# Where a modulation product stands between the matmuls of a two-layer trunk, and how its token sums are formed

## The chip, the cores and the metric

The kernel runs on one core of a Trainium2 chip. The metric is the device time of one execution in microseconds (us). Five engines work side by side, each through its own list of instructions in order: PE (matrix products, with PEld for its weight loads), DVE (the vector engine), ACT (the scalar engine), POOL (GpSimd) and SP, which here does nothing but issue transfers from memory. An engine that waits for a semaphore holds everything behind it in its own list.

## The reference

Two layers of a diffusion trunk work on 512 latent tokens and 256 context tokens of width 1024. Each layer takes six modulation vectors from a small product, mixes the tokens (convolution branch and differential attention, one output projection), and then runs a squared-ReLU MLP of width 4096:

```python
mx = (silu_c @ w_ada[i] + b_ada[i])[:, None, :]      # latent: 6 x 1024 numbers
mc = silu_cc @ w_ada[i] + b_ada[i]                   # context: the same weights
sx1, ax1, gx1, sx2, ax2, gx2 = jnp.split(mx, 6, axis=-1)
...
x = x + gx1 * y_x
x = x + gx2 * sqrelu_mlp(modulate(rmsnorm(x, norm2_g[i]), sx2, ax2), w_mlp1[i], w_mlp2[i])
h_ctx = h_ctx + gc2 * sqrelu_mlp(modulate(rmsnorm(h_ctx, norm2_g[i]), sc2, ac2), w_mlp1[i], w_mlp2[i])
```

The modulation of layer 1 depends on the conditioning alone, not on the tokens. It can be computed at any time before layer 1 begins.

## The kernel before, in words

Every product is done in three matmuls (L140 to L142, in `mm3`, or L149 and L152 in the order "low half last"): an operand is split into a rounded high part and the rest, and high by high, high by low and low by high are added up in PSUM. So every weight slab and every activation has to be split before PE may use it: the high part by ACT (a copy that rounds), the low part by a subtraction on DVE or POOL. In the traces a name with `h` or `hi` is a high part and one with `l` or `lo` a low part.

This case lies between the end of layer 0's token mixing and the start of layer 1. The stages, in order:

- **Output projection** (tiles `o`): the merged branches times `w_out`, 24 blocks of 128 channels by 256 tokens. DVE adds each block to the residual stream `X` (L1395), ACT and DVE sum its squares (`nsq_so`, `acc`). Each 256 tokens ("half" in the code, three of them) are then normalized by `norm_mod`: PE sums over channels (`nc_n`), DVE and POOL form the reciprocal root (`ms_n`; the power is on POOL, L347), DVE or ACT puts it on a diagonal (`dg_n`), PE spreads it over the partitions (`nb_n`, L357), and DVE, ACT and POOL write the normalized `h2hh` and `h2hl`.
- **First features** (tiles `f_0`): the first 512 of the 4096 hidden units, from slabs `w1`, in 8 blocks over latent tokens and 4 over context tokens. ACT squares them (`hidden`, L1494 to L1496; context blocks go through a buffer `fr`, of which there is one), DVE takes the low part into `F` (L1499).
- **Second product** (tiles `r`) of chunk 0, then for chunks 1 to 6 a product of seven block products instead of eight (Strassen, for the latent and context tokens cut at token 384, tiles `p`) and again the second product (`second_slots`). Strassen needs sums of token blocks, `TS` and a new `h2h` block, made once in `token_sums`: chains of additions into a buffer `G` (L1509), each chain ended by a split (L77).
- **Features of chunk 7** (tiles `f_7`), then **out slabs**: the last second product over 1024 hidden units in 24 blocks of 256 tokens (tiles `r` again, L140 to L142), with sums of squares and the first normalization of layer 1 (`norm1`: `nc_n_1`, `ms_n_1`, `dg_n_1`, `nb_n_1`, `h1h`, `h1l`), and then `qk`, the first product of layer 1.

**The modulation of layer 1** is `ada_rows`, a generator whose steps are called one by one (`ada_step`, `ada`). It goes through 12 pairs of slabs of `w_ada`, numbered s = 0, 2, ... 22, each in 8 rows of 128x512. A row is loaded by SP (tile `ar`, 256 KB, L299), the first row is scaled by ACT (L312), the other seven are multiplied and added by DVE (L314, into `adaac`, later into a piece of `G`), once for s of 8 and more, twice below it (latent and context). A pair ends with a transpose and a reduction on DVE (L323, L325) into `part`, and after s = 6 and s = 22 PE folds `part` (`adaps`, L288). There are 112 operations of L314 in all. Before the change the rows are kept in two buffers, the generator is first called beside first features, and it runs to its end beside the out slabs. `part` lies in the buffer `dg` of the pool `spool`, of which there is one; `dg_n` uses the same buffer.

**What sets the order.** A scheduler places the instructions of each engine by its own cost model. Where code stands in `with in_order():`, each engine's instructions keep the order in which they are written; every such block starts anew. Inside the chunks a table `PACE` says how many modulation steps (or, in chunk 0, token sums) follow each half block.

## Time and profile before

| | |
|---|---|
| median of 3 runs | 2345.85 us (2343.96 to 2348.31) |
| the profiled execution | 2341.43 us, span from first to last instruction 2339.7 us |
| PE busy | 2240.5 us, 96% of the span |
| DVE, ACT, POOL busy | 72%, 45%, 28% |
| layer 0's output projection | about 750 to 818 us |
| first features | 818 to 857 us |
| second product of chunk 0 | from 863 us |
| features of chunk 7 | 1256 to 1290 us |
| out slabs and first normalization of layer 1 | 1290 to 1380 us |

A row of the timeline reads: start in us, duration in us, engine, source line, operation, output tile <- input tiles, shapes, count; in brackets at its end, for how long the engine had been idle and who ended that. A row of the stage table reads: stretch, its length, and busy time with the number of instructions for PE, PEld, DVE, ACT and POOL; then PEclk, the mean clock that PE was granted (1.00 is full), the share of the transfer engines in use, and GB/s. A row of the table of waits reads: engine, tile and line that waited, the engine, tile and line that released it, total in us, how often, the longest.

### The profile page before, as it was taken

What the parts mean: (1) busy time and instruction counts of PE and PEld (TensorE: products, weight loads), DVE (VectorE), ACT (ScalarE), POOL (GpSimd) and SP (SyncE); (2) the same over time, 40 slices, a digit from 0 to 9 for tenths busy, and PEclk for the clock granted to TensorE, in tenths of its full rate; (3) what the DMA queues carried; (4) which work ended last, traced back from release to release, by engine and by line L of the source; (5) the groups of instructions that cost most, each with busy time, mean ns of one, the idle gap of its engine ahead of it and who ended that gap; (6) DMA issues with size and microseconds to landing.
All of it is one profiled execution on the core that took longest, in us unless ns stands there. A gap on an engine that the chain in (4) does not pass through costs nothing.

```text
span 2339.7 us, 36471 instructions
## 1 busy us (share of the span) xinstructions
PE 2240.5 (96%) x14402; PEld 2024.9 (87%) x14402; DVE 1683.5 (72%) x2754; ACT 1053.4 (45%) x2049; POOL 643.8 (28%) x781
## 2 busy tenths in 40 slices
PE   8999999999999979999999978999998999999999
PEld 6999998888888969999999878999987879888887
DVE  6777776599666477788676567777759976757673
ACT  5555654522332353343346235555543333655542
POOL 1866764110000131222122238576621000100000
PEclk9999999999999989999999989999999999999999
DMA  9211111134535131233344541112113423442251
GB/s 309 64 41 33 45 46 45 46 129 158 174 126 178 48 122 37 91 99 122 100 126 152 171 110 55 40 30 62 44 59 110 137 83 127 153 127 90 73 180 36
DMA packets 202266, 232.62 MB, mean 99 GB/s; under 512 B 8864, under 2 KB 162928, under 8 KB 201968
## 3 DMA queue, kind: packets, MB, share of 16 engines
q1 hardware_dynamic: 202096, 230.30, 31.1%
q8 instruction: 113, 1.85, 0.3%
q14 instruction: 57, 0.47, 0.1%
HBM read 212.93 MB, written 17.35 MB: 98 GB/s over the span
## 4 chain that ended last, share of the span: by engine, by line
PE 71%; DVE 12%; ACT 6%; POOL 4%; issue 3%; DMA 3%; SPq 0%; DVEq 0%; POOLq 0%; ACTq 0%
PE r L149 5%; PE gt L140 3%; PE gt L141 3%; PE gt L142 3%; PE r L141 3%; PE r L142 3%; PE r L140 3%; PE r L152 3%; PE f L141 3%; PE f L142 3%; PE f L140 3%; PE qk L140 2%; PE qk L141 2%; PE qk L142 2%; PE yc L149 2%
## 5 line engine op out<-in xcount | busy, mean ns | idle before, releaser
L1197 DVE SCALAR_TENSOR_TENSOR cacc<-z,cols,cacc 128x783 f32<-128x783 f32 (+1 forms) x240 | 208.3, 924 | 0.3
L140 PE MATMUL qk<-h_wqk,h1h 128*128 128x256 f32 x640 | 184.6, 291 | 4.3 <-ACT h1h L379 2.2
L141 PE MATMUL qk<-l_wqk,h1h 128*128 128x256 f32 x640 | 181.7, 286 | 0.0
L142 PE MATMUL qk<-h_wqk,h1l 128*128 128x256 f32 x640 | 176.6, 286 | 0.0
L961 DVE TENSOR_REDUCE st<-S 128x1 f32<-128x768 f32 (+1 forms) x160 | 134.5, 846 | 56.8 <-PE S L959 55.7
L964 ACT ACTIVATE e<-S,st 128x768 f32<-128x768 f32 (+1 forms) x160 | 130.9, 821 | 41.6 <-DVE st L961 40.6
L141 PE MATMUL f<-h2hl,h_w 128*128 128x512 f32 (+1 forms) x416 | 143.3, 346 | 1.3 <-POOL h2hl L77 1.2
L140 PE MATMUL f<-h2hh,h_w 128*128 128x512 f32 (+1 forms) x416 | 142.1, 347 | 1.1 <-ACT h2hh L76 1.0
L142 PE MATMUL f<-h2hh,l_w 128*128 128x512 f32 (+1 forms) x416 | 142.4, 344 | 0.0
L140 PE MATMUL gt<-h1h,h_wg 128*128 128x512 f32 (+1 forms) x384 | 138.2, 360 | 0.0
L141 PE MATMUL gt<-h1l,h_wg 128*128 128x512 f32 (+1 forms) x384 | 136.6, 356 | 0.0
L142 PE MATMUL gt<-h1h,l_wg 128*128 128x512 f32 (+1 forms) x384 | 136.6, 356 | 0.0
L149 PE MATMUL r<-F,whir 128*128 128x512 f32 (+1 forms) x384 | 125.7, 343 | 7.5 <-ACT whir L1548 6.2
L140 PEld LDWEIGHTS qk<-h_wqk,h1h 128*128 128x128 f32 x640 | 123.9, 194 | 7.9 <-ACT h1h L379 3.6
L149 PE MATMUL r<-F,wlor 128*128 128x512 f32 (+1 forms) x384 | 125.4, 342 | 3.2 <-DVE wlor L1551 1.9
L141 PEld LDWEIGHTS qk<-l_wqk,h1h 128*128 128x128 f32 x640 | 124.1, 194 | 0.3 <-POOL l_wqk L77 0.3
L142 PEld LDWEIGHTS qk<-h_wqk,h1l 128*128 128x128 f32 x640 | 120.9, 194 | 0.0
L140 PE MATMUL v<-h_wv,h1h 128*128 128x256 f32 x384 | 111.5, 290 | 6.6 <-ACT rwc L853 3.3
L142 PE MATMUL v<-h_wv,h1l 128*128 128x256 f32 x384 | 109.2, 284 | 0.0
L141 PE MATMUL v<-l_wv,h1h 128*128 128x256 f32 x384 | 108.7, 283 | 0.0
L795 POOL TENSOR_TENSOR rqk<-rqk,mhalf 128x4 f32<-128x4 f32 x80 | 86.0, 1078 | 79.1 <-DVE rqk L794 77.9
L957 PE MATMUL S<-qk 128*128 128x512 f32 (+1 forms) x288 | 101.8, 357 | 5.3 <-ACT e L964 4.7
(399 smaller groups left out, 7465.4 us busy)
## 6 DMA issues: line engine op xcount, KB each, us to landing
r_w<-in_w_mlp_dram SPq DMA_DIRECT2D x34, 1024.0 KB, 5.4
ada<-in_w_ada_dram SPq DMA_DIRECT2D x24, 1024.0 KB, 5.7
ar<-in_w_ada_dram SPq DMA_DIRECT2D x96, 256.0 KB, 2.9
r_wg<-in_w_in_dram SPq DMA_DIRECT2D x16, 1024.0 KB, 5.2
r_wqk<-in_w_in_dram SPq DMA_DIRECT2D x30, 512.0 KB, 5.2
rf<-in_w_mlp_dram SPq DMA_DIRECT2D x26, 512.0 KB, 3.7
rr<-in_w_mlp_dram SPq DMA_DIRECT2D x24, 512.0 KB, 3.5
r_wao<-in_w_attn_out_dram SPq DMA_DIRECT2D x8, 1024.0 KB, 5.1
```

What stands on the lines that cost most here:

```text
L140: nc.tensor.matmul(ps, sh, mh, start=first, stop=False)
L141: nc.tensor.matmul(ps, sh, ml, start=False, stop=False)
L142: nc.tensor.matmul(ps, sl, mh, start=False, stop=last)
L149: nc.tensor.matmul(ps, w[j][:, k, m0 : m0 + P], a(k)[0][:, toks], start=k + j == 0, stop=False)
L152: nc.tensor.matmul(ps, w[0][:, k, m0 : m0 + P], a(k)[1][:, toks], start=False, stop=k == nk - 1)
L795: nc.gpsimd.tensor_tensor(out=r, in0=r, in1=mhalf[:, :4], op=ALU.pow)
L957: nc.tensor.matmul(S[:, o], QH[:, m, ts], QH[:, 2 + m, lo:hi], start=True, stop=False)
L961: nc.vector.tensor_reduce(out=st[:, m : m + 1], in_=S[:, :nkey], axis=AX.X, op=ALU.max, negate=True)
L964: nc.scalar.activation(out=e[:, :nkey], in_=S[:, :nkey], func=AF.Exp, bias=st[:, m : m + 1], accum_out=st[:, 2 + m : 3 + m])
L1197: nc.vector.scalar_tensor_tensor(out=ca[cc][:, :CV], in0=zt[cc][:, t : t + CV], scalar=wcol, in1=ca[cc][:, :CV], op0=ALU.mult, op1=ALU.add)
```

## The change

1. `ada_rows` takes a list `early` of slab pairs that go first, here s = 0 and s = 8. They are called beside the output projection, one step or two behind each of the first 15 of its 24 blocks (`ada_beside`), with three row buffers (tag `ar`). None is called beside first features any more. The other ten pairs keep two buffers, and start in chunk 1.
2. `part` gets tiles of its own (`adp2`, `adp1`), so it no longer shares the buffer of `dg_n`.
3. `token_sums` forms its sums in another way: the sum of a block's high and low part is kept and used again. 9 additions and 4 low parts per half of the channels, where there were 10 and 4.
4. All `in_order` blocks from first features to chunk 7 share one dictionary, so the order is pinned across them too.
5. In chunk 0 all four low parts of the second product's slabs (`wlor`) are on DVE; three of them were on POOL. Three of the four loads for them are issued before first features.
6. `PACE` and the counts of steps beside the features of chunk 7 and the out slabs are set anew.

```diff
@@ in_order
-    def in_order():
+    def in_order(before):
...
-        before = {}
@@ ada_rows
-        plan = [(s, k) for s in range(0, 24, 2) for k in range(8)]
+        plan = [(s, k) for s in (*early, *(s for s in range(0, 24, 2) if s not in early))
+                for k in range(KT)]
...
+            tag, bufs = ("ar", 3) if s in early else ("araw", 2)
+            r = state["tp"].tile([P, 512], F32, tag=tag, bufs=bufs, name=f"ar{i}_{s}_{k}")
...
-                    part = spool.tile([P, 4, P], F32, tag="dg", bufs=1, name=f"adp{i}_{s}")[:, :, :32]
+                    parts[nq] = state["xp"].tile([P, 4, 32], F32, tag=f"adp{nq}", bufs=1,
+                                                 name=f"adp{i}_{s}")
@@ output projection
+        def ada_beside(*counts):
+            left = list(counts)
+            def tick():
+                for _ in range(left.pop(0) if left else 0):
+                    with tc.issue_after(state["done"]):
+                        next(ada_todo, None)
+            return tick
...
+            ada_todo = ada_rows(i + 1, Ln, (0, 8))
...
-                  (lambda: mlp1_slab(0, 0), lambda: mlp1_slab(0, 1)))
+                  (lambda: mlp1_slab(0, 0), lambda: mlp1_slab(0, 1)),
+                  None if last else ada_beside(*[1] * 10, 2, 2, 2, 2, 1))
@@ token_sums
-                    yield from sums(g0, f32(b12[0]), (less, b11[0]), (plus, b12[1]), (less, b11[1]))
-                    yield from sums(g1, f32(b22[0]), (less, b12[0]), (plus, b22[1]), (less, b12[1]))
+                    yield from sums(g0, (plus, *b12))
+                    yield from sums(g1, (less, b22[0], g0), (plus, None, b22[1]))
+                    yield from sums(g0, (less, None, b11[0]), (less, None, b11[1]))
                     split(*t1, g0)
                     yield
-                    yield from sums(g0, g1, (plus, b11[0]), (plus, b11[1]))
+                    yield from sums(g0, (less, b22[0], None), (plus, None, b22[1]))
                     split(*t3, g1)
@@ first features
+            for half in ((0, 0), (0, 1), (1, 0)):
+                load("r", 0, *half)
...
-                        if n:
-                            ada_step()
...
-                        sum_step((4, 4, 2, 0)[2 * s + m])
+                        sum_step((4, 3, 0, 1)[2 * s + m])
...
                             r0.fill(0, nc.vector)
-                            r0.fill(1, nc.gpsimd)
+                            r0.fill(1, nc.vector)
@@ chunks, chunk 7 and out slabs
-            PACE = {0: [(1, 1), (1, 1), (1, 1), (1, 1), (1, 1), (1, 1), (1, 2), (2, 1)],
+            PACE = {0: [(1, 1), (1, 1), (2, 1), (2, 1), (0, 1), (1, 0), (1, 2), (1, 1)],
...
-                        own = (ada,) if c > 2 else ()
+                        own = (ada,) if c > 1 else ()
...
+                    eng = nc.gpsimd if c else nc.vector
...
-                            ada((2, 2, 2, 2, 2, 2, 1, 0)[n])
+                            ada((2, 2, 2, 2, 2, 2, 0, 0)[n])
...
-                gate2, f"r{i}", norm1, after, tick=ada_step, ahead=
+                gate2, f"r{i}", norm1, after, tick=ada_beside(2, 2, *[1] * 10), ahead=
```

Lines below the edits are shifted: L1499 becomes L1512, L1509 becomes L1522, L1551 becomes L1565, L314 becomes L321, L1395 becomes L1400.

DVE around the end of first features, before (`adaac` is a modulation operation, `G` a token sum, `F<-fr` the low part of a context block, `wlor` a low part for the second product, `X` the first residual of that product):

```order
L1509 TENSOR_TENSOR G<-G,h2hl_8464 128x768
L314 SCALAR_TENSOR_TENSOR adaac_0_0_9452<-ar_0_5_9555,cvec,adaac_0_0_9452 128x512
L314 SCALAR_TENSOR_TENSOR adaac_0_1_9453<-ar_0_5_9555,cvec,adaac_0_1_9453 128x512
L77 TENSOR_TENSOR TS<-G,TS 128x768
L1551 TENSOR_TENSOR wlor_0_9763<-rr_0_0_9725,whir_0_9762 128x1024
L1499 TENSOR_TENSOR F<-fr_9729,F 128x256
L314 SCALAR_TENSOR_TENSOR adaac_0_0_9452<-ar_0_6_9588,cvec,adaac_0_0_9452 128x512
L314 SCALAR_TENSOR_TENSOR adaac_0_1_9453<-ar_0_6_9588,cvec,adaac_0_1_9453 128x512
L1509 TENSOR_TENSOR G<-G,h2hh_8463 128x768
L1499 TENSOR_TENSOR F<-fr_9729,F 128x256
L1395 SCALAR_TENSOR_TENSOR X_8450<-r_0_512_9802,ad_143,X_8450 128x256
```

and of the change, from the fourth sum to the last low part:

```order
L1522 TENSOR_TENSOR G<-G,h2hh_8463 128x768
L1512 TENSOR_TENSOR F<-fr_9697,F 128x256
L1522 TENSOR_TENSOR G<-G,h2hl_8464 128x768
L77 TENSOR_TENSOR TS<-G,TS 128x768
L1522 TENSOR_TENSOR G<-h2hh_8463,G 128x768
L1512 TENSOR_TENSOR F<-fr_9697,F 128x256
L1565 TENSOR_TENSOR wlor_0_9796<-rr_0_0_9459,whir_0_9795 128x1024
L1565 TENSOR_TENSOR wlor_0_9796<-rr_0_1_9461,whir_0_9795 128x1024
L1512 TENSOR_TENSOR F<-fr_9765,F 128x256
L1522 TENSOR_TENSOR G<-G,h2hl_8464 128x768
L1512 TENSOR_TENSOR F<-fr_9765,F 128x256
```

Twelve modulation operations that stood among the sums are gone from DVE there, and both `wlor` of the first slab stand ahead of the last two low parts.

POOL at the second normalization of layer 0, before (`l_w_0_0_0` and `l_w_0_0_1` are the low parts of the two slabs of first features, `ms_n_0_256` is the power for tokens 256 to 511):

```order
L77 TENSOR_TENSOR h2hl_8464<-nu_n_0_0_7_9033,h2hh_8463 128x256
L77 TENSOR_TENSOR l_w_0_0_0_9262<-r_w_0_0_0_9259,h_w_0_0_0_9261 128x1024 x2
L347 TENSOR_TENSOR ms_n_0_256_9157<-ms_n_0_256_9157,mhalf 128x2
L77 TENSOR_TENSOR l_w_0_0_1_9328<-r_w_0_0_1_9325,h_w_0_0_1_9327 128x1024 x2
L77 TENSOR_TENSOR h2hl_8464<-nu_n_0_256_1_9169,h2hh_8463 128x256
```

and of the change:

```order
L77 TENSOR_TENSOR l_w_0_0_0_9332<-r_w_0_0_0_9329,h_w_0_0_0_9331 128x1024 x2
L77 TENSOR_TENSOR h2hl_8464<-nu_n_0_0_7_9103,h2hh_8463 128x256
L77 TENSOR_TENSOR l_w_0_0_1_9398<-r_w_0_0_1_9395,h_w_0_0_1_9397 128x1024 x2
L352 TENSOR_TENSOR ms_n_0_256_9227<-ms_n_0_256_9227,mhalf 128x2
L77 TENSOR_TENSOR h2hl_8464<-nu_n_0_256_1_9239,h2hh_8463 128x256
```

The power for tokens 256 to 511 now stands behind both low parts of the second slab, where it stood ahead of them.

DVE at the end of the out slabs, before (`X<-r_7_512` is the last residual, `dg_n_1_0` and `nu_n_1_0` belong to layer 1's normalization of tokens 0 to 255):

```order
L314 SCALAR_TENSOR_TENSOR G<-ar_22_7_13958,cvec,G 128x512
L323 STREAM_TRANSPOSE adat_22_0_13962<-G 128x512
L1395 SCALAR_TENSOR_TENSOR X_8450<-r_6_512_14388,ad_143,X_8450 128x256
L325 TENSOR_REDUCE adp_8_12166<-adat_22_0_13962 128x4x4
L1395 SCALAR_TENSOR_TENSOR X_8450<-r_7_512_14417,ad_143,X_8450 128x256
L290 TENSOR_TENSOR ad_8498<-adaps_8_13965,cols_8470 128x32
L346 TENSOR_SCALAR ms_n_1_0_14111<-nc_n_1_0_14108 128x2
L337 SCALAR_TENSOR_TENSOR A_8500<-ad_8498,cols_8470 128x8
L353 TENSOR_SCALAR dg_n_1_0_14114<-cst,ms_n_1_0_14111 128x128 x2
L375 SCALAR_TENSOR_TENSOR nu_n_1_0_0_14119<-X_8450,A_8499,nb_n_1_0_14117 128x256
```

and of the change, at the same normalization:

```order
L1400 SCALAR_TENSOR_TENSOR X_8450<-r_7_0_14079,ad_143,X_8450 128x256
L400 TENSOR_TENSOR G<-G,nsq_sr_0_7_14105 128x256
L1400 SCALAR_TENSOR_TENSOR X_8450<-r_4_256_14155,ad_143,X_8450 128x256
L351 TENSOR_SCALAR ms_n_1_0_14111<-nc_n_1_0_14108 128x2
L1400 SCALAR_TENSOR_TENSOR X_8450<-r_5_256_14184,ad_143,X_8450 128x256
L358 TENSOR_SCALAR dg_n_1_0_14114<-cst,ms_n_1_0_14111 128x128 x2
L1400 SCALAR_TENSOR_TENSOR X_8450<-r_6_256_14213,ad_143,X_8450 128x256
L380 SCALAR_TENSOR_TENSOR nu_n_1_0_0_14119<-X_8450,A_8499,nb_n_1_0_14117 128x256
```

The normalization of tokens 0 to 255 stood behind all 24 residuals and the last modulation operation. It now stands behind the 17th residual (`r_4_256`), and the last modulation operation (on `ar_22_7`) right behind the 8th (`r_3_0`). On PE, the spread `nb_n_1_0` moves from behind the last block into the 20th (`r_7_256`, after 5 of its 24 matmuls), with four whole blocks and most of that one still to come. For tokens 256 to 511, `nc_n_1_256` and `nb_n_1_256` stood together behind the first 48 matmuls of layer 1 (`qk`). Now `nc_n_1_256` stands three matmuls before the end of the last block, and `nb_n_1_256` behind the first 31 matmuls of `qk`.

More of the change, by code (lines that the diff above doesn't have):

```diff
@@ L293, in fold, with load @@
                 .to_broadcast([P, nq, 2 * ns]), op=ALU.add)
[L295 to L298 removed]
+        plan = [(s, k) for s in (*early, *(s for s in range(0, 24, 2) if s not in early))
+                for k in range(KT)]
+        waiting, parts = [], {}
+        def load(n):
+            s, k = plan[n]
+            tag, bufs = ("ar", 3) if s in early else ("araw", 2)
+            r = state["tp"].tile([P, 512], F32, tag=tag, bufs=bufs, name=f"ar{i}_{s}_{k}")
             nc.sync.dma_start(r, rows(w_ada[i], 256 * s, 512)[:, k])
[L300 to L302 removed]
+            waiting.append(r)
+        ahead = 0
         for n, (s, k) in enumerate(plan):
             nq = 2 if s < 8 else 1
+            end = len(early) * KT if s in early else len(plan)
+            while ahead < min(n + (3 if s in early else 2), end):
+                load(ahead)
+                ahead += 1
             if k == 0:
                 if s in (0, 8):
[L307 removed]
+                    parts[nq] = state["xp"].tile([P, 4, 32], F32, tag=f"adp{nq}", bufs=1,
+                                                 name=f"adp{i}_{s}")
+                part = parts[nq]
                 acc_ = [t2k(f"adaac{i}_{s}_{q}") for q in range(nq)]
@@ L316, in ada_rows @@
                         op0=ALU.mult, op1=ALU.add)
-            if n + 2 < len(plan):
-                waiting.append(load(*plan[n + 2]))
             if k == KT - 1:
@@ L1479, in trunk_kernel @@
             T2 = B12
-            ada_todo = ada_rows(i + 1, Ln)
-            def ada_step():
-                with tc.issue_after(state["done"]):
-                    next(ada_todo, None)
             def hidden(cch, s, m, g, f, x):
@@ L1505, in token_sums, with sums @@
                     nc.sync.dma_start(b12_d[j], f32(B12[j]))
-                def sums(t, first_, *terms):
-                    for op, b in terms:
-                        tt(out=t, in0=first_, in1=f32(b), op=op)
-                        first_ = t
+                def sums(t, *terms):
+                    for op, a_, b_ in terms:
+                        tt(out=t, in0=t if a_ is None else f32(a_),
+                           in1=t if b_ is None else f32(b_), op=op)
                         yield
@@ L1776, in ada @@
                     next(ada_todo, None)
-            with in_order():
+            with in_order(chain):
                 for c in range(7):
@@ L1857, in trunk_kernel @@
                         at(6), at(7)])
-                    if c == 0:
-                        drain(sums)
                     tail = (late2, nothing)
-            with in_order():
+            with in_order(chain):
                 rest, n = None, 0
```

30 lines of the change are left out of this document (13 added, 17 removed), and 7 rows, old and new, of the table PACE.

## The prediction

> **What bounds the kernel now.** I read the page's shares of busy time first.
>
> ```profile
> span 2339.7 us, 36471 instructions
> PE 2240.5 (96%) x14402; PEld 2024.9 (87%) x14402; DVE 1683.5 (72%) x2754; ACT 1053.4 (45%) x2049; POOL 643.8 (28%) x781
> ```
>
> PE has 99.2 us in which it does not multiply, in the whole program. A change that leaves PE's products alone can win only from that idle time and from time at a lowered clock, so the second view is the table of stages around the edits.
>
> ```profile
> core 0: us, PE busy (x) PEld busy (x) DVE busy (x) ACT busy (x) POOL busy (x), PEclk, DMA share, GB/s
> 750.00:818.00 68.00, 68.00 (x568) 67.95 (x568) 31.30 (x64) 19.90 (x40) 8.28 (x7) 1.00 0.28 95
> 818.00:857.00 39.00, 37.60 (x303) 36.50 (x301) 25.99 (x53) 26.18 (x65) 13.09 (x13) 1.00 0.30 98
> 857.00:880.00 23.00, 8.98 (x32) 7.20 (x33) 19.43 (x20) 8.41 (x13) 9.43 (x3) 0.63 0.45 144
> 880.00:912.00 32.00, 32.00 (x184) 28.57 (x183) 27.94 (x40) 7.52 (x12) 1.30 (x1) 1.00 0.00 1
> 912.00:1256.00 344.00, 341.86 (x1959) 319.83 (x1958) 267.51 (x407) 145.96 (x260) 72.12 (x38) 1.00 0.34 107
> 1256.00:1297.00 41.00, 36.23 (x213) 31.59 (x211) 22.25 (x22) 23.94 (x40) 15.54 (x6) 1.00 0.56 178
> 1297.00:1345.00 48.00, 46.73 (x375) 46.55 (x376) 28.92 (x44) 11.40 (x21) 10.16 (x4) 0.96 0.54 173
> 1345.00:1400.00 55.00, 42.12 (x300) 39.18 (x298) 38.22 (x69) 18.97 (x40) 15.78 (x15) 0.88 0.51 119
> ```
>
> The output projection (750 to 818) and the chunks (880 to 1256) have a full PE and a clock of 1.00. The idle time sits in three seams, and the clock falls right behind them. I count as lost by the clock a stage's PE busy time x (1 - PEclk).
>
> - Seam A, first features to second product (857:880): idle 23.00 - 8.98 = 14.0, clock 8.98 x 0.37 = 3.3. Together 17.3 us.
> - Seam B, features of chunk 7 to out slabs: idle 41.00 - 36.23 = 4.8, clock behind it 46.73 x 0.04 = 1.9. Together 6.7 us.
> - Seam C, out slabs to layer 1 (1345:1400): idle 55.00 - 42.12 = 12.9, clock 42.12 x 0.12 = 5.1. Together 18.0 us.
>
> These 42 us are all that the change can reach here. Third, the waits of PE in seams A, B and C say who is late:
>
> ```profile
> PE r L149 <- ACT whir L1548: 6.2, 1, 6.2
> PE r L152 <- DVE F L1499: 5.0, 1, 5.0
> PE r L149 <- DVE wlor L1551: 1.9, 1, 1.9
> PE r L149 <- POOL wlor L1551: 1.3, 1, 1.3
> ...
> PE r L141 <- DVE TS L1499: 4.2, 1, 4.2
> ...
> PE nb_n L357 <- DVE dg_n L353: 5.3, 2, 3.6
> PE r L140 <- DVE X L1395: 4.4, 5, 1.3
> PE qk L140 <- ACT h1h L379: 2.2, 2, 1.1
> PE adaps L288 <- DVE adp L325: 1.0, 1, 1.0
> ```
>
> DVE stands behind nearly all of it, and in each seam modulation operations stand ahead of the one that PE wants.
>
> **Seam A.** The timeline at first features, by start, duration and engine:
>
> ```profile
> 847.55 0.96 DVE L1509 TENSOR_TENSOR G<-h2hh 128x768 f32<-128x768 f32 x1
> ...
> 861.72 1.99 ACT L1548 ACTIVATE whir<-rr 128x1024 fp32r<-128x1024 f32 x2
> 862.82 0.58 PE L149 MATMUL r<-F,whir 128*128 128x256 f32 x1 [6.20 <-ACT whir L1548]
> 863.84 9.43 POOL L1551 TENSOR_TENSOR wlor<-rr,whir 128x1024 fp32r<-128x1024 f32 x3 [16.82 <-ACT whir L1548]
> 863.99 1.22 DVE L1551 TENSOR_TENSOR wlor<-rr,whir 128x1024 fp32r<-128x1024 f32 x1
> 865.46 5.62 DVE L314 SCALAR_TENSOR_TENSOR adaac<-ar,cvec,adaac 128x512 f32<-128x512 f32 x2
> ...
> 874.01 0.41 DVE L1499 TENSOR_TENSOR F<-fr,F 128x256 fp32r<-128x256 f32 x1
> ```
>
> PE is out of features at 862.82 - 6.20 = 856.6, and the last low part `F` ends at 874.4, 26.9 us after the first token sum on DVE (847.55). ACT's `whir` comes late for the same reason: it stands behind squares that wait for the single `fr`, which DVE frees. The change removes the modulation from this list: two operations of 2.81 us each in the row at 865.46, and others before it, on rows that were still landing. It also takes POOL's three `wlor`, 9.43 us, to DVE. By the new order DVE does, from its first sum on: four sums (0.96 each), one `F` (0.41), one sum, one split (a pass on ACT and a subtraction, taken as two sums' time), one sum, one `F`: 8 x 0.96 + 2 x 0.41 = 8.5. Then two `wlor` (2 x 1.22), `F`, one sum, `F`: 4.2. The last `F` then ends at 847.55 + 12.7 = 860.3, 14.1 earlier; `whir` ends before PE's features do. PE is out of features at 856.6, and has the K0 half of its first blocks, for which everything is there, before it needs the last `F`. I take 3.0 us of idle and 0.9 of clock as what stays: 17.3 - 3.9 = **-13.4**. Bounds: -16.5 (nothing waits but 0.8), and -10 (3.7 us of ACT's squares between `whir` and the last `F` stay in the way).
>
> **A new wait (D).** The three first loads for the second product now stand on SP before first features, which costs nothing there. But POOL's order has changed at layer 0's second normalization:
>
> ```profile
> 819.01 0.70 POOL L347 TENSOR_TENSOR ms_n<-ms_n,mhalf 128x2 f32<-128x2 f32 x1 [0.49 <-DVE ms_n L346]
> 819.67 4.75 POOL L77 TENSOR_TENSOR l_w<-r_w,h_w 128x1024 fp32r<-128x1024 f32 x2
> ...
> 823.22 0.59 PE L357 MATMUL nb_n<-dg_n,cst 128*128 128x256 f32 x2
> ...
> 825.00 0.50 PE L140 MATMUL f<-h2hh,h_w 128*128 128x256 f32 x2
> ```
>
> The power `ms_n` for tokens 256 to 511 ran ahead of the two `l_w`; it now runs behind them. They begin at about 819.3, when ACT has their high part, so the power runs from 824.0 to 824.7. With a diagonal of 0.7 `nb_n` comes at 825.4, and `f`, which followed `nb_n` by 1.8, at 827.2 instead of 825.0. Behind it waits all of first features for tokens 256 to 511. **+3.0**: 2.2 of idle and 0.8 of clock. Bounds: 0 (PE still has features of tokens 0 to 255 to do) and +5.
>
> **Seam B.** The two rows that end it:
>
> ```profile
> 1292.02 2.20 DVE L314 SCALAR_TENSOR_TENSOR adaac<-ar,cvec,adaac 128x512 f32<-128x512 f32 x1 [0.89 <-DMA ar<-in_w_ada_dram]
> 1294.14 2.82 DVE L1499 TENSOR_TENSOR TS<-G,TS 128x512 fp32r<-128x512 f32 x1
> ```
>
> The low part `TS` that PE waits for 4.2 us stands behind a modulation operation that itself waited 0.89 for its row. The counts 1, 0 at the last two blocks become 0, 0, so that operation goes; two pairs of operations beside the block before stay in front. Gone are 0.89 + 2.20 = 3.1; of the idle time 4.8 - 3.1 = 1.7 stays, and I leave 0.8 of the clock's 1.9: 6.7 becomes 2.5, **-4.2**. Bounds: -6.5 and -0.2 (the subtraction itself took 2.82, and may still).
>
> **Seam C.**
>
> ```profile
> 1365.38 5.73 POOL L77 TENSOR_TENSOR l_wqk<-r_wqk,h_wqk 128x1024 fp32r<-128x1024 f32 x2 [28.27 <-ACT h_wqk L76]
> ...
> 1375.23 2.56 DVE L353 TENSOR_SCALAR dg_n<-cst,ms_n 128x128 f32<-128x128 f32 x2 [0.74 <-POOL ms_n L347]
> ```
>
> `dg_n` shares its one buffer with `part`, which is read for the last time after the last modulation operation. So the normalization of tokens 0 to 255, whose sums are complete 16 blocks into the 24, came behind everything. With `part` in a tile of its own, `nb_n_1_0` is inside the 20th block and four more blocks hide it. Of the four waits of PE, the 3.6 of `nb_n` and the 1.0 of `adaps` go (4.6); of the 4.4 for `X` most goes too, since 8 modulation operations stand beside the out slabs instead of 26; of the 2.2 for `h1h` about half. What is late next is `nb_n` for tokens 256 to 511: POOL's two `l_wqk` now stand ahead of its power. They began in time for that (1365.38 + 5.73 = 1371.1, the last block ends at 1374), and 31 matmuls of `qk` lie ahead on PE. I leave 2.0 of idle and 1.0 of clock: 18.0 - 3.0 = **-15.0**. Bounds: -17.5, and -9 (`l_wqk` late by 5.73, with the clock behind it).
>
> **Where the modulation goes.** Prices and landing times:
>
> ```profile
> L314 DVE SCALAR_TENSOR_TENSOR adaac<-ar,cvec,adaac x91: 735/746/2895, 845.0 to 1311.1; 128x512 f32<-128x512 f32 x91
> ...
> ar<-in_w_ada_dram SPq DMA_DIRECT2D x96, 256.0 KB, 2.9
> X<-xs_d SPq DMA_DIRECT2D x8, 384.0 KB, 6.7
> ```
>
> Beside the output projection come 21 operations (7 rows twice, 7 once) of 0.746 = 15.7 us, and three transposes with reductions of about 1.4 a pair = 4.2. DVE is busy 31.3 of 68 us there and PE does not wait: 51.2 of 68, hidden, 0. Without that cover it would be 20 us. The 16 rows go through SP ahead of the second slab of first features: its issue comes at about the 12th of the 24 blocks, some 30 us ahead of 818, and such a load lands within 6.7: hidden. In chunk 0 as many sums are left as before, and two `wlor` are added (2.4): 27.94 + 2.4 of 32.00, thin cover, 0. Chunks 1 to 7 take 73 + 10 operations instead of 65 + 9; 8 x 0.746 = 6.0 us on a DVE that is busy 267.51 of 344, 0. The token sums themselves shrink by one of 0.96 per half, off PE's path.
>
> **The sum**: -13.4 + 3.0 - 4.2 - 15.0 = -29.6. The profiled execution took 2341.43; it becomes 2311.8. That execution lies 4.4 below the median of the runs, 2345.85, so I forecast 2316.2, say **2316**.
>
> A rule of the Trainium skill bears on the clock terms. "TensorE: Matmul & The Clock Gate" (What's actually happening; Why this matters for your kernels) says that the clock halves after an idle window of about 3.4 us and asks for no gaps beyond about 3 us. By it the short gaps that I leave in A, D and C would lose no clock. The trace has a row that speaks against it:
>
> ```profile
> 1380.00:1400.00 20.00, 17.07 (x104) 16.20 (x104) 15.49 (x34) 13.32 (x34) 7.04 (x11) 0.75 0.38 42
> ```
>
> PE was idle 2.93 in all of these 20 us and was granted 0.75. So short gaps in a row do cost clock here, and I keep these terms.
>
> **Rivals.**
>
> 1. No clock is lost at the short gaps: the terms 0.9, 0.8 and 1.0 fall away, 2.7 us, so 2313.5. For it: PE's clock in the stage 818:857 is 1.00 with 1.4 idle. Against it: the row just shown. This is the result that the skill's rule would give. 12%.
> 2. Seam C keeps its wait. POOL's `l_wqk`, 5.73, starts late against an out-slab stage that is now shorter (it waits for ACT's `h_wqk`, whose slab has its time from a load), and the power of tokens 256 to 511 and the next `nb_n` with it. C then gives 3 instead of 15: 2316 + 12 = 2328. For it: `dg_n` and `l_wqk` on their two engines already took 2.56 and 2.87 each here. Against it: four blocks of cover for the first half. 15%.
> 3. DVE becomes the bound of chunk 0. It had 4.1 us to spare in 880:912, and an operation beside POOL or DMA can take 2.895 instead of 0.746. Five sums at 2.1 us more overrun by 10.5 - 1.7 = 8.8: 2325. Against it: POOL's `wlor`, beside which the slow rows stood, are gone. 8%.
> 4. Slower: beside the output projection DVE waits in order for rows, and the residuals `X` behind it free PSUM for the blocks. With three buffers 16 rows come at a third of a landing time t each, against 15 blocks of 68 / 24 = 2.8 = 43 us. PE waits from t = 43 x 3 / 16 = 8 us on; it is slower than before once 16 t / 3 exceeds 43 + 29.6, that is from t = 13.6 us; at 15 us 80 - 43 - 29.6 = +7.5, so 2353. For it: the residual stream `X` is read in the same stage, 6.7 us a load. Against it: rows land in 2.9. 5%.
> 5. The change doesn't do what it says: PE's wait at seam A passes to ACT's `whir` or squares and seam C's to `h1h`, and both keep their length. 2345. Against it: both stand behind DVE's rows now. 3%.
>
> **How the numbers follow.** The forecast as worked out gets 57%, with its own range of 2308 to 2325. The bounds of the unknown terms added up give -16.5 - 6.5 - 17.5 = -40.5, which is 2305, and -10 + 5 - 0.2 - 9 = -14.2, which is 2332; rivals 1 to 3 lie inside. So the range is 2304 to 2332, and about 2 in 10 is left for the ends and for rivals 4 and 5. A measurement here tells about 0.2% from no change, 4.7 us. Faster: 57 + 12 + 15 + 8 = 92%. Same: 3%. Slower: 5%.
>
> **What would show it.** Right: the stage of seam A has PE idle of about 3 instead of 14.0; no `F` released by DVE costs PE over 2 us; `nb_n` waits for `dg_n` once, for under 2 us; the stage of the output projection keeps PE full. Step D is right if `f` of tokens 256 to 511 follows POOL's second `l_w`, and wrong if the stage 818:857 still has 1.4 idle. Wrong: waits of PE for `o`'s PSUM behind `X` (rival 4), for `TS` at the start of chunk 1 (rival 3), a POOL `l_wqk` that ends after the last block (rival 2).

## The result, and the profile after

The changed kernel takes 2315.86 us, median of 4 runs (2313.95 to 2318.08), against 2345.66 for the kernel before (4 runs, 2343.96 to 2348.31): a ratio of 0.9872, 95% interval 0.9855 to 0.9889, or 29.8 us. The forecast was 2316, 29.6 less in the sum of its terms. So much agreement in the total asks for a look at the terms, and one of them came near its size for a reason that did not hold.

The profiled execution of the change took 2318.08, the slowest of its four runs, and its page begins

```profile
span 2316.3 us, 36447 instructions
PE 2240.6 (97%) x14402; PEld 2025.7 (87%) x14402; DVE 1677.2 (72%) x2755; ACT 1055.7 (46%) x2049; POOL 633.6 (27%) x778
```

PE's busy time is the same to 0.1 us, so the 23.4 us by which the span fell (2339.7 to 2316.3) are idle time of PE. What the seams won back in clock (PE's busy time in seam C fell from 42.12 to 36.31) was lost again in other stages. The table of stages of the change has the columns of the one in the prediction, and its edges are the same places in PE's work. One edge is set more sharply: the end of PE's first features, which lay at 856.6 before. The other edges moved by 0.1 at most. Before, the two stages at this edge were

```profile
818.10:856.60 38.50, 37.48 (x302) 36.40 (x300) 25.59 (x53) 26.18 (x65) 12.99 (x13) 1.00 0.30 98
856.60:880.10 23.50, 9.10 (x34) 7.30 (x34) 19.93 (x21) 8.41 (x13) 9.43 (x3) 0.64 0.45 143
```

and in the change the table is

```profile
core 0: us, PE busy (x) PEld busy (x) DVE busy (x) ACT busy (x) POOL busy (x), PEclk, DMA share, GB/s
752.80:820.80 68.00, 68.00 (x568) 67.95 (x567) 47.88 (x89) 21.60 (x42) 7.58 (x6) 1.00 0.52 172
820.80:862.80 42.00, 39.01 (x302) 37.58 (x300) 25.87 (x53) 26.93 (x68) 13.56 (x14) 0.96 0.11 39
862.80:872.10 9.30, 7.32 (x32) 6.08 (x33) 7.90 (x11) 6.46 (x9) 0.00 (x0) 0.82 0.50 161
872.10:904.10 32.00, 32.00 (x184) 28.57 (x183) 29.22 (x41) 8.23 (x13) 1.30 (x1) 1.00 0.07 21
904.10:1252.40 348.30, 343.44 (x1959) 320.93 (x1959) 273.88 (x413) 147.39 (x263) 71.83 (x38) 1.00 0.36 115
1252.40:1292.10 39.70, 36.46 (x213) 31.61 (x211) 18.41 (x23) 21.52 (x36) 10.02 (x4) 1.00 0.61 191
1292.10:1338.10 46.00, 46.00 (x376) 45.82 (x377) 28.25 (x42) 12.21 (x24) 15.10 (x6) 0.96 0.40 119
1338.10:1375.00 36.90, 36.31 (x300) 35.82 (x298) 21.61 (x49) 18.73 (x43) 15.11 (x15) 1.00 0.38 110
```

DVE carries 47.9 us of work beside the output projection instead of 31.2, and the stage is still 68.0 long with a full PE. Set against the stages before, with two further profiles of the same program (below), in us:

| term | forecast | first profile | second | third |
|---|---|---|---|---|
| seam A, first features to second product | -13.4 | 9.3 - 23.5 = -14.2 | -13.6 | -13.8 |
| new wait D, first features | +3.0 | 42.0 - 38.5 = +3.5 | +4.4 | +4.2 |
| seam B, with the clock behind it | -4.2 | 85.7 - 89.1 = -3.4 | -3.1 | -3.2 |
| seam C, out slabs to layer 1 | -15.0 | 36.9 - 55.0 = -18.1 | -18.1 | -18.1 |
| chunks 1 to 6 | 0 | 348.3 - 343.9 = +4.4 | +0.8 | +0.8 |
| output projection and chunk 0 | 0 | 0 | +1.0 | +1.0 |
| sum | -29.6 | -27.8 | -28.6 | -29.1 |

The span fell by 4.4 less than these stages (27.8), since the mixing of layer 0 and layer 1, whose work the change leaves alone, were 2.7 and 1.7 us longer in the first profile of the change. PE was busy 3.0 and 2.1 us longer there with the same matmuls: that is half clock, which falls differently from profile to profile (last section). The median fell by 29.8 all the same, because the profiled execution before (2341.43) lay 4.2 below its median and that of the change (2318.08) 2.2 above.

What PE still waits for in the change, in first features (with POOL's rows there), around seam B and in the chunks, and two rows of the timeline at B's wait:

```profile
PE nb_n L362 <- ACT dg_n L356: 1.6, 1, 1.6
PE f L139 <- ACT h2hh L384: 1.2, 1, 1.2
...
822.99 4.74 POOL L77 TENSOR_TENSOR l_w<-r_w,h_w 128x1024 fp32r<-128x1024 f32 x2 [0.88 <-ACT h_w L76]
827.69 0.70 POOL L352 TENSOR_TENSOR ms_n<-ms_n,mhalf 128x2 f32<-128x2 f32 x1
...
PE r L139 <- ACT TS L1508: 1.6, 1, 1.6
PE r L140 <- DVE TS L1512: 1.0, 1, 1.0
...
PE r L148 <- ACT F L1647: 4.0, 5, 2.1
...
1288.79 0.72 ACT L319 ACTIVATE G<-ar,cvec 128x512 f32<-128x512 f32 x1 [9.24 <-DMA ar<-in_w_ada_dram]
...
1290.71 0.38 PE L139 MATMUL r<-TS,h_w 128*128 128x256 f32 x1 [1.63 <-ACT TS L1508]
```

In first features the power of tokens 256 to 511 runs when POOL's two subtractions end. At seam C 0.6 is left of the 12.9. At B the wait no longer begins with DVE: the first row of slab pair s = 22 is scaled by ACT, ACT had been idle for 9.24 when that row landed, and the squares that PE wants stand right behind it in ACT's list.

### The profile page after: what moved, and what is told of

It is laid out like the page before. It is cut to its first block, busy times and chain, and to the rows that moved or that the text cites. A ratio compares the mean times of both kernels' runs of the same rounds, so it can differ in the third digit from the quotient of the medians.

```text
span 2316.3 us, 36447 instructions
## 1 busy us (share of the span) xinstructions
PE 2240.6 (97%) x14402; PEld 2025.7 (87%) x14402; DVE 1677.2 (72%) x2755; ACT 1055.7 (46%) x2049; POOL 633.6 (27%) x778
## 4 chain that ended last, share of the span: by engine, by line
PE 72%; DVE 11%; ACT 6%; POOL 5%; DMA 4%; issue 2%; SPq 0%; DVEq 0%; ACTq 0%; POOLq 0%
PE r L148 4%; PE r L140 3%; PE r L141 3%; PE r L139 3%; PE gt L139 3%; PE gt L140 3%; PE gt L141 3%; PE f L140 3%; PE f L139 3%; PE f L141 3%; PE r L151 2%; PE qk L139 2%; PE qk L140 2%; PE qk L141 2%; DMA ar<-in_w_ada_dram 2%
## 5 line engine op out<-in xcount | busy, mean ns | idle before, releaser
L321 DVE SCALAR_TENSOR_TENSOR adaac<-ar,cvec,adaac 128x512 f32<-128x512 f32 x105 | 100.3, 975 | 32.0 <-DMA ar<-in_w_ada_dram 31.8
```

The costliest lines, as they stand in the source:

```text
L321: nc.vector.scalar_tensor_tensor(out=a, in0=r, scalar=cvec[:, k, q : q + 1], in1=a, op0=ALU.mult, op1=ALU.add)
```

## The experiments

### The changed kernel again, twice

No edit.

> The changed kernel once more, a second profile of the same program. Theory of the prediction: the seams shrink by the same amounts as in the first profile of the change (A -14.1, D +3.0, B -3.4, C about -17), since these are waits in program order. Rival: part of the difference of the first profile was a matter of where the windows at half clock fell; then the half-clock windows behind the short idle times at 646, 1186 and 1425 us come and go from one profile to the next, 1.7 us each, and the span differs by some 2 to 5 us while PE's idle time stays within 1 us.

> The changed kernel a third time, as the partner of the version with three more edits on one chip: median 2316 to 2319. Theory of the half-clock windows: idle time of PE at the seams within 0.3 of the first profile, and half clock behind each window of 3.4 us in which PE stood for about half or more.

Measured: 2315.87 (2315.09 to 2319.41), ratio 0.9879 (0.9856 to 0.9902), and 2316.39 (2314.80 to 2319.07), ratio 0.9872 (0.9856 to 0.9888). The chunks, from the tables of stages of the second and the third profile:

```profile
908.40:1253.10 344.70, 341.81 (x1959) 319.75 (x1959) 269.63 (x412) 146.93 (x262) 72.41 (x38) 1.00 0.36 116
...
904.00:1248.70 344.70, 341.83 (x1959) 319.76 (x1959) 271.35 (x411) 146.30 (x261) 72.55 (x38) 1.00 0.36 115
```

The terms at the seams come back within 0.9 us. In the chunks the wait at 994 (1.4) is there each time; that at 1186 (2.1, and half clock behind it) was in the first profile alone. The expected 0.3 was too narrow: the idle time of first features is 3.0, 3.0 and 3.6.

### The partial sums in a tile of their own, and nothing else

```diff
@@ before: ada_rows
-  part = spool.tile([P, 4, P], F32, tag="dg", bufs=1, name=f"adp{i}_{s}")[:, :, :32]
+  part = state["xp"].tile([P, 4, 32], F32, tag=f"adp{nq}", bufs=1, name=f"adp{i}_{s}")
```

> The kernel before, with the partial sums of the modulation in a tile of their own instead of the buffer of the normalization's diagonal, and nothing else. Theory of the prediction for seam C: the shared buffer held the first normalization of layer 1 back, so about -15 (2331). Rival: what holds it back is that the modulation itself, 26 operations beside the out slabs and the product that folds them, ends late; the tile alone then gives 0 (2345), with PE's four waits at that seam unchanged.

Measured: 2348.28 (2342.86 to 2352.84, 10 runs), ratio 1.0009 (0.9995 to 1.0022): nothing. Its seam C (55.0 before), and what PE waits for in it:

```profile
1348.00:1405.80 57.80, 43.61 (x299) 41.04 (x298) 39.79 (x69) 19.02 (x41) 15.19 (x15) 0.85 0.49 112
...
PE r L140 <- DVE X L1396: 6.7, 5, 3.7
PE nb_n L358 <- DVE dg_n L354: 5.3, 2, 3.6
PE qk L140 <- ACT h1h L380: 2.2, 2, 1.1
```

The wait for `dg_n` is the same 5.3 as before. No engine's list of instructions differs from the kernel before: the first normalization of layer 1 stands behind the last modulation operation with or without the shared buffer. The theory of the shared buffer falls.

### The modulation ends earlier, and the buffer stays shared

```diff
@@ before: chunks
-  1: [(0, 1), (1, 0), (1, 1), (1, 0), (0, 0), (0, 0), (1, 0), (1, 1)],
-  2: [(0, 1), (1, 0), (1, 1), (1, 1), (0, 0), (0, 0), (1, 0), (1, 1)],
-  3: [(0, 1), (1, 0), (1, 1), (1, 1), (0, 0), (0, 1), (1, 1), (1, 1)],
-  4: [(1, 1), (1, 1), (1, 1), (1, 1), (0, 0), (0, 1), (1, 1), (1, 1)]}
+  1: [(1, 1), (1, 1), (1, 1), (1, 1), (0, 0), (0, 1), (1, 1), (1, 1)],
+  4: [(1, 1), (1, 1), (1, 2), (1, 1), (0, 1), (0, 1), (1, 1), (1, 1)]}
+  PACE[2] = PACE[3] = PACE[1]
...
-  own = (ada,) if c > 2 else ()
+  own = (ada,) if c > 1 else ()
```

> The kernel before, with 17 more modulation steps in the chunks and as many fewer beside the out slabs; the buffer stays shared and seam A stays as it was. Theory of the prediction for seam C (the shared buffer): the diagonal still waits for the end of the modulation, so C gives at most a third, -5 (2341). Rival (the end of the modulation): C shrinks by the 15 to 17 us that the change brought there (about 2330), less what the additional steps cost in the chunks, 0 to 4 us.

Measured: 2323.46 (2321.71 to 2326.18), ratio 0.9906 (0.9879 to 0.9933). Chunks, seam B, the out slabs and seam C:

```profile
916.50:1262.00 345.50, 342.49 (x1958) 319.98 (x1958) 275.39 (x423) 146.47 (x261) 71.23 (x38) 1.00 0.37 118
1262.00:1299.30 37.30, 36.15 (x213) 31.60 (x212) 17.76 (x22) 23.92 (x41) 11.76 (x5) 1.00 0.59 193
1299.30:1345.20 45.90, 44.64 (x377) 44.30 (x376) 31.50 (x47) 11.34 (x22) 13.86 (x6) 1.00 0.53 172
1345.20:1382.50 37.30, 36.50 (x300) 35.92 (x298) 23.40 (x49) 18.80 (x42) 15.08 (x15) 1.00 0.30 86
```

Seam C falls from 55.0 to 37.3, nearly all that the change got there, and B with the clock behind it from 89.1 to 83.2, more than in the change. The 17 steps cost 1.6 in the chunks; seam A, untouched, was 24.2. So it is the end of the modulation that C waits for, and the rival is right. It also means that about 22 of the change's 30 us are to be had from the places of the steps in the chunks alone.

### One slab pair back beside first features

```diff
@@ after: output projection, first features
-  ada_todo = ada_rows(i + 1, Ln, (0, 8))
+  ada_todo = ada_rows(i + 1, Ln, (8,))
...
-  None if last else ada_beside(*[1] * 10, 2, 2, 2, 2, 1))
+  None if last else ada_beside(*[1] * 9))
...
   hidden(0, s, m, g, F, GF[:, 256 * (n % 6) : 256 * (n % 6) + 256])()
+  if n:
+      with tc.issue_after(state["done"]):
+          next(ada_todo, None)
```

> The change with the slab pair s = 0 taken back from the output projection to first features, where it is called step by step as in the kernel before (12 operations); the pair s = 8 stays beside the output projection, and three steps go on to later places. Theory: at seam A these operations stand ahead of the last low parts again, so A loses what the change gained there through modulation, 8 to 13 us of the 14 (2324 to 2329); the rest of A came from the low parts wlor and the sums. Rival: A's gain came from the order of the sums and of wlor, and A loses less than 4 (under 2320).

Measured: 2323.57 (2322.74 to 2326.95), ratio 0.9912 (0.9889 to 0.9934). Seam A and its wait:

```profile
858.70:874.40 15.70, 7.77 (x34) 6.45 (x33) 12.79 (x19) 8.54 (x13) 0.00 (x0) 0.67 0.41 127
...
PE r L148 <- ACT whir L1562: 7.3, 1, 7.3
```

Seam A is 15.7 instead of 9.3 to 9.9: 6 us, between what theory and rival gave. But the stage in front of it changed too:

```profile
820.20:858.70 38.50, 37.48 (x302) 36.40 (x300) 26.74 (x55) 25.46 (x64) 12.99 (x13) 1.00 0.23 76
...
821.11 0.70 POOL L352 TENSOR_TENSOR ms_n<-ms_n,mhalf 128x2 f32<-128x2 f32 x1 [0.49 <-DVE ms_n L351]
```

POOL does the power first again here (its two `l_w` follow at 821.77), the new wait D is gone, and first features take 38.5 as before the change. So PE comes to the seam 3.5 to 4.4 us sooner, and part of its longer wait there is time that it lost in front of the seam in the change. First features and seam A together took 62.0 before, 51.3 to 52.8 in the three profiles of the change, and 54.2 here. The pair beside first features thus cost 1.4 to 2.9 us over both stages, much less than half of A's 14. The rest of the 7.7 by which the median is longer lies elsewhere: in the profile the chunks took 350.4 (344.7 to 348.3 in the change), and from the end of seam C to the end of the program it took 946.1 (941.3 to 941.6).

### Three low parts back on POOL

```diff
@@ after: first features, chunk 0
-  r0.fill(1, nc.vector)
+  r0.fill(1, nc.gpsimd)
...
-  eng = nc.gpsimd if c else nc.vector
+  eng = nc.gpsimd
```

> The change with the low parts wlor of the second product's slabs in chunk 0 back on POOL where they were (three of four); order of sums and modulation as in the change. Putting the slab pair s = 0 back beside first features cost 6.3 at seam A of the 14.1 that the change gained there, so 7.8 came from elsewhere. Theory: from wlor, which took 9.43 for three on POOL beside a busy DVE; then A loses 5 to 8 (2321 to 2324). Rival: with DVE idle of modulation POOL's wlor is fast enough (2.4 each alone) and hidden behind the K0 half; A loses under 2 (2316 to 2318), and the 7.8 came from the order of the sums behind the low parts F.

Measured: 2324.88 (2321.05 to 2329.38), ratio 0.9916 (0.9891 to 0.9942).

```profile
863.40:879.50 16.10, 8.61 (x33) 6.97 (x34) 12.16 (x9) 6.55 (x9) 7.94 (x3) 0.68 0.43 130
...
865.39 7.94 POOL L1565 TENSOR_TENSOR wlor<-rr,whir 128x1024 fp32r<-128x1024 f32 x3 [13.03 <-ACT whir L1562]
865.49 2.60 DVE L1512 TENSOR_TENSOR F<-fr,F 128x256 fp32r<-128x256 f32 x1
...
PE r L151 <- DVE F L1512: 4.2, 1, 4.2
PE r L148 <- POOL wlor L1565: 1.5, 1, 1.5
```

Seam A is 16.1: 6 to 7 us lost with the modulation gone, as expected. POOL needs 7.94 for three operations; DVE's busy time in the seam is 12.16 for 9 instructions, where the change has 7.90 for 11. PE's longer wait is for DVE's last `F`, not for POOL: while the three `wlor` run, DVE's next three operations take 2.60, 3.12 and 2.57 us, where the same three take 0.42, 0.95 and 0.42 in the change. This also bears on the two modulation operations of 2.81 at seam A before, which ran beside POOL's `wlor`: in the version above, where POOL has none, two such operations took 1.40 together. First features and seam A together are 59.3 here, 6.5 to 8.0 more than in the change. So over both stages `wlor` holds most of the gain and the modulation the smaller part.

### The token sums in the old way

```diff
@@ after: token_sums
-  yield from sums(g0, (plus, *b12))
-  yield from sums(g1, (less, b22[0], g0), (plus, None, b22[1]))
-  yield from sums(g0, (less, None, b11[0]), (less, None, b11[1]))
+  yield from sums(g0, f32(b12[0]), (less, b11[0]), (plus, b12[1]), (less, b11[1]))
+  yield from sums(g1, f32(b22[0]), (less, b12[0]), (plus, b22[1]), (less, b12[1]))
...
```

> The change with the token sums formed in the old way (10 additions per half of the channels instead of 9), all else as in the change. Theory: one addition of 0.96 per half is off PE's path, and the number of sums ahead of the last low part is the same; 0 to +1 at seam A, 2316. Rival: the sums are on the path through chunk 0 to the first Strassen product of chunk 1; then PE waits there for TS and it costs 2 to 4 (2318 to 2320).

Measured: 2319.19 (2317.00 to 2319.35), ratio 0.9889 (0.9868 to 0.9911). Seam A and chunk 0:

```profile
865.90:875.40 9.50, 7.64 (x34) 6.11 (x34) 7.94 (x11) 5.58 (x8) 0.00 (x0) 0.82 0.51 166
875.40:908.10 32.70, 32.24 (x184) 28.48 (x182) 30.29 (x41) 7.38 (x12) 1.30 (x1) 1.00 0.09 26
```

Nothing at A, 0.7 in chunk 0, where DVE is busy 30.29 of 32.70: the cover there is as thin as the prediction had it. The times alone can't tell it from the change.

### The power ahead of the second slab

```diff
@@ after: rstd_bcast, norm2, load of the second slab
+  state["pow"] = nc.gpsimd.tensor_tensor(..., op=ALU.pow).ins    # kept for tokens 256 to 511
...
+  state["behind"] = (*state["behind"], state["pow256"])          # the splits of the slab come behind it
   mlp1_slab(0, 1)
```

> The change with the second slab of first features split behind the power of tokens 256 to 511, so that POOL does the power first, as in the kernel before. Theory (the new wait D): PE's two waits of 1.59 and 1.18 at 828 to 831 and the half-clock window behind them go, -3.0 (2313). Rival: the slab's low parts are then late by what the power gained, and PE waits for l_w instead: within 1 of the change (2316).

Measured: 2320.93 (2314.13 to 2323.07), ratio 0.9902 (0.9876 to 0.9928): no gain to be seen in the times. The profiled execution is the fastest of the four. In it first features take 40.0 instead of 42.0 to 42.9:

```profile
818.70:858.70 40.00, 37.69 (x302) 36.28 (x300) 25.71 (x53) 26.82 (x68) 13.52 (x14) 1.00 0.11 41
```

The wait for the diagonal, 1.6, is gone, and the half clock with it; the wait of 1.2 for ACT's `h2hh` stays. Seam A was 11.0 in this profile, with two half-clock windows instead of one, so that the whole comes to little.

### A third pair beside the output projection

```diff
@@ after: output projection, chunks 4 and 5
-  ada_todo = ada_rows(i + 1, Ln, (0, 8))
+  ada_todo = ada_rows(i + 1, Ln, (0, 8, 10))
...
-  None if last else ada_beside(*[1] * 10, 2, 2, 2, 2, 1))
+  None if last else ada_beside(*[1] * 10, *[2] * 9))
...
-  4: [(1, 1), (1, 1), (1, 2), (1, 1), (0, 1), (0, 1), (2, 1), (2, 1)]}
+  4: [(1, 1), (1, 1), (1, 1), (1, 1), (0, 0), (0, 1), (1, 1), (1, 1)]}
```

> The change with a third slab pair (s = 10, 9 steps) beside the output projection, and 8 steps fewer in chunks 4 and 5, where the change had added them. Theory: in those chunks the added modulation operations made the last features of the next chunk late (PE waits 2.07 for them at 1186, and a half-clock window in one of two profiles); these go, -2 to -4 (2312 to 2314), and the output projection stays full, since DVE has 16 us left there. Rival: beside the output projection DVE is now late with the residuals, PE waits there for PSUM, and the time is the change's or more (2316 to 2325).

Measured: 2315.11 (2313.21 to 2317.13), ratio 0.9874 (0.9852 to 0.9896), level with the change. First features, the chunks and seam B:

```profile
820.70:865.00 44.30, 39.63 (x302) 37.98 (x300) 27.07 (x54) 27.26 (x69) 14.35 (x14) 0.92 0.10 37
...
907.90:1254.20 346.30, 343.40 (x1959) 320.90 (x1958) 267.87 (x405) 146.21 (x262) 71.50 (x38) 1.00 0.34 110
1254.20:1290.70 36.50, 35.90 (x213) 31.60 (x212) 18.12 (x22) 22.01 (x37) 10.82 (x5) 1.00 0.64 207
```

The wait at 1186 is gone, the one at 994 stays and now has half clock behind it. Seam B is 36.5 instead of 39.7. A first row still stands ahead of the last squares on ACT, but it lands 32.5 us into the stage instead of 36.4, and PE does not wait for it any more. First features pay 1.4 to 2.3 for it.

### No step beside the features of chunk 7

```diff
@@ after: chunk 7
-  ada((2, 2, 2, 2, 2, 2, 0, 0)[n])
+  ada(0)
```

> The change with no modulation step beside the features of chunk 7; the 12 steps go to the out slabs, where 20 operations then stand instead of 8 (26 before the change). The end of the modulation moves behind the 17th residual, just ahead of the first normalization of layer 1, which still comes four blocks before the end. Theory (the order at the end of the modulation decides seam C, not the number of operations beside the out slabs): C stays within 1 us of the change, and B falls by the 2 to 3 of idle that a late row there still costs, since no row is waited for in front of the last squares. Rival: 20 operations keep DVE late with the residuals, PE waits for X beside the out slabs as before the change (4.4), and C or the out slabs lose 4 to 8.

Measured: 2319.41 (2317.41 to 2321.89), ratio 0.9882 (0.9866 to 0.9899). Seam B and seam C, and C's waits:

```profile
1250.00:1287.20 37.20, 36.21 (x214) 31.69 (x213) 6.58 (x11) 22.48 (x38) 11.30 (x5) 1.00 0.37 119
...
1332.20:1375.30 43.10, 38.57 (x299) 36.57 (x298) 27.53 (x58) 19.16 (x43) 15.23 (x15) 0.96 0.31 90
...
PE r L139 <- DVE X L1400: 2.3, 1, 2.3
PE qk L139 <- ACT h1h L384: 1.1, 1, 1.1
```

B gives 2.5 as expected, but C loses 6.2 (43.1 against 36.9) though the normalization keeps its place ahead of the last four blocks. The expectation for C fell and the rival's loss of 4 to 8 came: DVE waits 6.8 us in all for rows of the modulation to land, the residual `X` stands behind them, and PE waits 2.3 for it. Seam C has two parts: when the modulation ends, and how many rows DVE still has to wait for in front of the residuals.

### Three fixes together

The edits of "the power ahead of the second slab" and "a third pair", and one step more in chunk 1, which moves the first row of s = 4 away from the split of the second product's slab in chunk 2:

```diff
-  1: [(0, 1), (1, 0), (1, 1), (1, 0), (0, 0), (0, 1), (1, 0), (1, 1)],
+  1: [(1, 1), (1, 0), (1, 1), (1, 0), (0, 0), (0, 1), (1, 0), (1, 1)],
```

> The change with three more edits: POOL's power of tokens 256 to 511 ahead of the second slab's low parts; the third slab pair beside the output projection with 8 steps fewer in chunks 4 and 5; and one step more in the first slot of chunk 1, so that the first row of slab pair s = 4, which ACT scales, no longer stands ahead of the split of the second product's slab in chunk 2 (a wait of PE of 1.4 at 994). Theory: these waits fall one by one where the profile has them: the first of the two at 828 (1.6), the ones at 994 (1.4), 1186 (2.1) and 1289 to 1292 (2.6), together 7.7 of idle, and about three half-clock windows of 1.7: span 2305 to 2309 against 2316 and 2318 in the two profiles of the change. Rival: the fixes move the same waits to other places (the output projection, the second step of chunk 2), and the span stays above 2311.

Measured: 2310.97 (2307.78 to 2315.67, 5 runs), ratio 0.9853 (0.9835 to 0.9872), beside 2316.39 for the change on the same chip. Chunks and seam B:

```profile
903.10:1247.10 344.00, 341.88 (x1960) 319.77 (x1958) 269.37 (x406) 146.49 (x262) 72.24 (x38) 1.00 0.35 112
1247.10:1283.60 36.50, 35.90 (x214) 31.65 (x213) 18.45 (x23) 22.57 (x38) 10.85 (x5) 1.00 0.61 199
```

The chunks are back at 344.0, what they took before the change; B keeps 0.6 of idle, and with the additional step no first row stands ahead of its last squares; the span is 2306.0, as expected, in the fastest of the five runs. The median is 5.4 lower than the change's, and the two ratios' intervals overlap, so that this is likely rather than certain; the waits that went are seen one by one.

### Stops of PE of known length

```diff
@@ after: second_slots, chunks 1 to 5, ten places, n = 2, 4, 5, 6 or 8
+  nc.tensor.matmul(ps[:, :P], ones, ident, start=True, stop=True)
+  nc.scalar.activation(out=gz[:, :P], in_=ps[:, :P], func=AF.Copy)
+  for _ in range(n - 1):
+      nc.scalar.activation(out=gz, in_=cst[:, :256], func=AF.Copy)
+  nc.tensor.matmul(ps[:, 256 : 256 + P], ones, gz[:, :P], start=True, stop=True)
```

> The change with ten additional stops of PE in the chunks, where PE is otherwise full: after the sixth or second block of a second product (chunks 1 to 5) PE makes a small product, ACT copies 2, 4, 5, 6 or 8 times, and PE makes a small product from the last copy; each length twice, all of it additional to the computation. Lengths by ACT's copies of 0.4: about 0.9, 1.7, 2.1, 2.5 and 3.3 us. Theory (half clock follows a window of 3.41 us of the fixed grid in which PE stood for about half or more): never behind 0.9, always or nearly always behind 3.3, behind 1.7 to 2.5 according to how the stop falls on the grid. Rival (only a window without any work, 3.4 us, lowers the clock, and no stop under 3): half clock behind none of the stops up to 2.5.

Measured: one run, 2350.91; the stops took 21.9 us in all. Three of the ten stops, and the clock in the window behind each of them, in the same order:

```profile
1016.49 0.49 PE L1728 MATMUL gap<-gz,cst 128*128 128x128 f32 x2 [1.71 <-ACT gz L1727]
1179.40 0.49 PE L1728 MATMUL gap<-gz,cst 128*128 128x128 f32 x2 [1.77 <-ACT gz L1727]
1252.92 0.49 PE L1728 MATMUL gap<-gz,cst 128*128 128x128 f32 x2 [2.22 <-ACT gz L1727]
...
1016.50:1019.90 3.40, 3.40 (x22) 3.10 (x23) 2.12 (x4) 0.00 (x0) 0.00 (x0) 1.00 0.75 236
1180.40:1183.80 3.40, 3.40 (x13) 3.01 (x12) 2.13 (x4) 0.72 (x1) 0.00 (x0) 0.50 0.32 96
1252.10:1255.50 3.40, 2.58 (x18) 2.46 (x19) 2.01 (x5) 1.46 (x3) 0.00 (x0) 1.00 0.45 146
```

In this trace the clock changes only at edges that lie a multiple of 3.413 us apart. With each stop cut at these edges:

| stop, us | largest piece in one window | clock in the next |
|---|---|---|
| 0.81, 0.87 | 0.81, 0.87 | full |
| 2.22 | 1.36 (and 0.86) | full |
| 1.71 | 1.71 | full |
| 1.77 | 1.77 | half |
| 2.16 | 1.99 | half |
| 2.61 | 2.11 | half |
| 2.67 | 2.67 | half |
| 3.56, 3.50 | 3.10, 3.23 | half |

Half of a window is 1.71. A stop of 2.22 that an edge cuts in two left the clock alone; one of 1.77 within a window halved it.

## Why the prediction was right, and where it was not

- **What bounds the kernel**: right. PE's busy time stayed at 2240.6 and the gain came from the three seams; the output projection stayed full under 16.7 us more of DVE's work, but for one wait of 0.7 in the second and the third profile.
- **Seam A**, -13.4 against -13.6 to -14.2: right in size, and both causes that it names are real: at the seam, taking back one slab pair cost 6 and taking `wlor` back to POOL 6 to 7. It did not weigh them against each other. It took the 2.81 of a modulation operation there as the price of the modulation, though its rival 3 notes that such slow rows stood beside POOL's `wlor`, and without those two such operations took 1.40; over first features and the seam together `wlor` was worth 6.5 to 8.0 and the pair 1.4 to 2.9. One step failed in the small: "`whir` ends before PE's features do". PE waited 1.0 for it, and DVE 2.38, so that DVE's chain from the first sum to the last `F` took 14.6 (853.05 to 867.66) instead of 12.7. The rest that I left, 3.0 of idle, was 2.0 in the first profile (`whir` 1.0, `wlor` 0.9); the last `F` is no longer among PE's longer waits.
- **The new wait D**, +3.0 against +3.5 to +4.4: right in its cause for the larger part, and some 1 us too small. With the power first the stage is 2.0 to 2.9 shorter; 1.5 more than before the change remain, and there PE's longest wait is the 1.2 for `h2hh`, which the forecast did not have. The two `l_w` began at 822.99, 2.2 behind the end of the output projection at 820.8, where I had taken 1.2.
- **Seam B**, -4.2 against -3.1 to -3.4: a little too large, since I looked at DVE alone. What stayed was ACT's scaling of a first row that had not landed.
- **Seam C**, -15.0 against -18.1: the step that failed is "`dg_n` shares its one buffer with `part` ... So the normalization of tokens 0 to 255 ... came behind everything". The tile of its own gives nothing; an earlier end of the modulation gives 17.7 with the buffer shared. The forecast came out right since the change does both, and since its other argument, fewer modulation operations beside the out slabs, was the one that held. I had read a shared tag in the code as the cause without asking whether the list of instructions would differ without it. The size was too small by the 3.0 that I left for POOL's `l_wqk`, which was not late.
- **The cover in the chunks**, 0 against +0.8 to +4.4: the step that DVE is busy "267.51 of 344" hides an average. The operations stand ahead of chains that PE meets within a us or two: 1.4 at 994 each time, 2.1 at 1186 once. In the version with three fixes both are gone.
- **The rivals**: no half clock at short stops (2313.5) is refuted, as the stops of known length show. C's wait on POOL, DVE as the bound of chunk 0, and late rows beside the output projection did not occur; the mechanism of the last did occur beside the out slabs, in the version without steps beside chunk 7, at 2.3 us. (In rival 2, the 2.56 of `dg_n` is two operations together, not one.)
- That the median fell on the forecast to 0.2 us is partly luck. C gave 3.1 more than forecast and A 0.2 to 0.8 more; D, B, the chunks and the output projection together gave 4.0 to 5.7 less, and these errors cancel. Three profiles of one program also lie between 2313.0 and 2317.6 in span.

## What to carry to other kernels

Where a side task shares an in-order engine with the chain that PE waits for, its place is the stage with a full PE and a half idle engine; what counts is how many of its operations stand ahead of the one that PE meets at a seam, and when it ends, not how busy the engine is on average. Before a shared buffer is called a cause, part it alone and see whether the order of any engine changes: here the one-line edit settled it. Several of the waits that the change left (a first row on ACT, a power behind two subtractions) were each one row in front of the wanted one, and moving steps of the side task or one operation of POOL removed them. And where an edit shortens one stage and lengthens the next, read the two together: the 6 us that one slab pair cost at seam A were mostly time that PE had won in the stage in front of it.
